# Seven-product blocks that sum in PSUM: ScalarE copies partial sums from bank to bank, TensorE adds onto them, VectorE keeps one addition per block

## The chip, the cores and the metric

The kernel runs on one core of a Trainium2 chip. The metric is the device time of one execution in microseconds. The core has four computing engines with a queue each: TensorE (PE; its weight loads are listed as PEld), VectorE (DVE), ScalarE (ACT) and GpSimd (POOL). SyncE (SP) issues most of the DMAs. Matrix products land in PSUM, which the kernel uses as eight banks of 128 partitions by 512 fp32 numbers; everything else lies in SBUF.

## The reference

A two-layer network on 512 tokens of width 1024. Each layer mixes tokens (layer A by chunked spatial gating, layer B by forgetting attention; both add attention to a memory of 256 rows) and then runs a gated feed-forward part of hidden width 2816 (22 blocks of 128):

```python
for layer in range(DEPTH):
    a = rmsnorm(h, ln_mix_pre[layer])
    ...
    mixed = jnp.concatenate([main, memory_attention(q_mem, mem_n, w_mem_kv[layer])], axis=-1)
    h = h + rmsnorm(mixed @ w_out[layer], ln_mix_post[layer])
    f = rmsnorm(h, ln_ffn_pre[layer])
    f = (jax.nn.silu(f @ w_ffn_gate[layer]) * (f @ w_ffn_up[layer])) @ w_ffn_down[layer]
    h = h + rmsnorm(f, ln_ffn_post[layer])
return h
```

The change is in the two products `f @ w_ffn_gate` and `f @ w_ffn_up`.

## The kernel before

Activations are held transposed: features on the partitions, tokens along the free dimension. An fp32 number is held as two parts, a high one that ScalarE makes by a rounding copy and a low one, the rest, that VectorE makes by a subtraction (`split`, line 239). A product of such pairs is three matmuls (`mm3`, lines 191 to 193): high by high, low weights or low data in the other two.

**Blocks of seven products.** Of the 22 hidden blocks of a layer, the first two are computed plainly. The other 20 go in ten pairs, and each pair is computed once for the gate weights and once for the up weights: 20 times per layer an object of the class `Seven`. It treats its piece of work as a product of 2x2 block matrices: two hidden blocks by two halves of the 1024 input features (the weight quadrants a11, a12, a21, a22, 128x512 each), times two halves of the features by two halves of the tokens. The four results take seven block products in place of eight, with additions before (`sums`: four VectorE additions on the weights; `combined`: the same on the data, once per layer) and additions behind. Each block product is four feature tiles times three matmuls, 12 matmuls with a 128x128 weight tile and 256 tokens.

With P1 to P7 for the products, the first hidden block gets P1 + P2 on the left tokens and P1 + P6 + P5 + P3 on the right ones; the second gets P1 + P6 + P7 + P4 and P1 + P6 + P7 + P5 (kept with the opposite sign, which the next step undoes).

**How the sums are made before.** A block has three PSUM tiles in three banks: `x` (512 wide; P2 in the left half, P3 in the right), `a` (`self.p`, 256 wide, in which P1, P6 and P5 are added up) and `e` (`self.q`, 256 wide; P7, then P4 on top). ScalarE copies four partial sums to SBUF tiles `s1` and `s2`, at lines 1059 (P1), 1074 (P7), 1071 (P1 + P6) and 1068 (P1 + P6 + P5). The products run in the order 1, 7, 2, 6, 4, 3, 5. In `end`, VectorE adds `e` and `a` onto the halves of `s2` (lines 1079 and 1080, 256 wide) and `x` onto `s1` (line 1082, 512 wide), and hands each finished row of 512 to `rows`: `gate_rows` multiplies by the norm factors and applies Silu, `up_rows` multiplies by the gate and splits the result into high and low parts for the down product.

**Where things wait for each other.** PSUM tiles come from pools by tag: `mm` (3 banks, the gate blocks), `lg` (3 banks, the up blocks) and `tr` (2). Weight parts come from a ring of 8 pairs of SBUF tiles (tags `hi` and `lo`); a block needs 7 pairs. The program writes the blocks one after the other; the framework's planner sets each engine's order at build time and the semaphores between engines, and it may put a later instruction ahead of an earlier one. The first pair of each layer (`plain_first`) runs its gate and up blocks interleaved, in the order 1, 2, 3, then 7, 6, then 4, 5. After each group of two or three pairs the down product for that group follows (tiles `y`), with 512-wide matmuls; its weights use the same ring.

Of the kernel before, what the change touches and what calls it, by code (L numbers as in the profile page):

```python
# [11 lines left out]
ALU = mybir.AluOpType  # L12
# [3 lines left out]
P = 128  # L16
# [17 lines left out]
HALVES = ((0, 256), (256, 512))  # L34
FULL = (0, 512)

ORDER = (6, 7, 0, 1, 2, 3, 4, 5)
# [3 lines left out]
def hybrid(ctx: ExitStack, tc: tile.TileContext, i: dict, out: bass.AP):  # L41
# [13 lines left out]
    def name(s):  # L55
        n_of[s] = n_of.get(s, 0) + 1
        return f"{s}_{n_of[s]}"
# [7 lines left out]
    def prob(s, shape=(P, T)):  # L65
        return tp.tile(list(shape), F32, tag="p", name=name(s), bufs=6)
# [7 lines left out]
    def ps(tag, shape=(P, T), s="ps"):  # L74
        return pp.tile(list(shape), F32, tag=tag, name=name(s), bufs=2 if tag == "tr" else 3)

    V, A, PE, G = nc.vector, nc.scalar, nc.tensor, nc.gpsimd
# [160 lines left out]
    def split(src, hi, lo, eng=None):  # L238
        last_parts[:] = A.copy(hi, src), (eng or V).tensor_sub(lo, src, hi)  # L239
# [22 lines left out]
    class Norm:  # L262


        def __init__(self, width=T):
            self.r4 = small("r4")
            self.acc, self.width = None, width
# [750 lines left out]
    class Seven:  # L1018
# [5 lines left out]
        def __init__(self, xs, src, tag, rows):  # L1024
            self.xs, self.rows = xs, rows
            w1, w2 = loaded(src(0)), loaded(src(1))
            self.a = [w[:, d : d + 512] for w in (w1, w2) for d in (0, 512)]
            self.x, self.p = ps(tag, s="x"), ps(tag, (P, 256), s="a")
            self.q = ps(tag, (P, 256), s="e")
            self.s1, self.s2 = prob("s1"), prob("s2")  # L1030

        def parts(self, src):
            pair = pair_of_parts()
# [14 lines left out]
        def product(self, o, w, n, more=False):  # L1048
            for k, w in enumerate(cut(w, P)):
                mm3(o, w, self.xs[n][k], k == 0 and not more, k == KT // 2 - 1, more)  # L1050

        def run(self, what):

            a11, a12, a21, a22 = self.a
            left, right = (slice(*c) for c in HALVES)
            s1, s2 = self.s1, self.s2
            if what == 1:
                self.product(self.p, self.w1, 0)
                A.copy(s1[:, left], self.p)
            elif what == 2:  # L1060
                self.product(self.x[:, left], self.w2, 2)
            elif what == 3:
                self.product(self.x[:, right], self.parts(a12), 5)
            elif what == 4:
                self.product(self.q, self.parts(a22), 4, True)
            elif what == 5:
                self.product(self.p, self.parts(a21), 6, True)
                A.copy(s1[:, right], self.p)
            elif what == 6:
                self.product(self.p, self.parts(a11), 3, True)  # L1070
                A.copy(s2[:, left], self.p)
            else:
                self.product(self.q, self.parts(self.s3), 1)
                A.copy(s2[:, right], self.q)

        def end(self):
            left, right = (slice(*c) for c in HALVES)
            s1, s2 = self.s1, self.s2
            V.tensor_add(s2[:, left], self.q, s2[:, left])
            V.tensor_add(s2[:, right], self.p, s2[:, right])  # L1080
            self.rows(1, s2)
            end = V.tensor_add(s1, self.x, s1)
            self.rows(0, s1)
            ended[0] = end

    ended = [None]

    def sevens(pair, plain_first, opens=False):

        if not plain_first:  # L1090
            for make in pair:
                u = make()
                with behind(ended if opens else ()):
                    u.sums()
                opens = False
                for n in (1, 7, 2, 6, 4, 3, 5):
                    u.run(n)
                u.end()
            return
        us = []  # L1100
        for make in pair:
            us.append(make())
            us[-1].sums()
            for n in (1, 2, 3):
                us[-1].run(n)
        for some in ((7, 6), (4, 5)):
            for u in us:
                for n in some:
                    u.run(n)
        for u in us:  # L1110
            u.end()

    def feed_forward(layer, phase, xp, meanwhile=None):

        nnorm = PairNorm()
        rb = rbc
        groups = ((2, 8), (8, 14), (14, 18), (18, 22))

        def hidden(gate, up, f, cols):
            c0, c1 = cols  # L1120
            n = c1 - c0
            gr = temp("gr")
            V.tensor_mul(gr[:, :n], gate, rb[:, c0:c1])
            s = temp("silu")
            A.activation(s[:, :n], gr[:, :n], AF.Silu)
            ff = temp("f")
            V.tensor_mul(ff[:, :n], up, s[:, :n])
            split(ff[:, :n], f[0][:, c0:c1], f[1][:, c0:c1])

        gates = [None] * 3  # L1130

        def gate_rows(row, g):

            V.tensor_mul(g, g, rb)
            gates[2] = A.activation(g, g, AF.Silu, scale=-1.0 if row else 1.0)
            gates[row] = g

        def up_rows(row, u, fs):
            if row:
                V.scalar_tensor_tensor(out=u, in0=u, scalar=-1.0, in1=gates[1], op0=ALU.mult, op1=ALU.mult)  # L1140
            else:
                V.tensor_mul(u, u, gates[0])
            split(u, *fs[len(fs) - 2 + row])

        fs = [(act("fhi"), act("flo")) for _ in range(2)]

        def first(n, aside):
            return prepared(i["w_up" if n % 2 else "w_gate"][layer, n // 2], (KT, P), aside)

        def evac_first(outs, cols):  # L1150
            for m in range(2):
                hidden(outs[2 * m], outs[2 * m + 1], fs[m], cols)

        scaled = {}
        a, close = boundary(phase, G_MIX_POST + layer, G_FFN_PRE + layer, nnorm, rb, first, evac_first, scaled)
        w = [down_weights(layer, 0, dh) for dh in range(2)]
        close()
        xs, last = combined(a, scaled, xp)
        last()
        ys = [[plain("y") for _ in range(2)] for _ in range(TB)]  # L1160
        for tb in range(TB):
            for dh in range(2):
                o = ps("lg" if dh else "mm", s="y")
                for k in range(2):
                    token_products(o, fs[k], w[dh][k], tb, k == 0, k == 1)
                A.copy(ys[tb][dh], o)

        for gi, (k0, k1) in enumerate(groups):
            fs = []
            for m in range(k0, k1, 2):  # L1170
                if meanwhile and m == k1 - 2 and gi == len(groups) - 1:
                    next(meanwhile)
                fs += [(act("fhi"), act("flo")) for _ in range(2)]
                sevens((lambda: Seven(xs, lambda n: i["w_gate"][layer, m + n], "mm", gate_rows),
                        lambda: Seven(xs, lambda n: i["w_up"][layer, m + n], "lg",
                                      lambda row, t: up_rows(row, t, fs))), m == 2, m == k0)
            nk = k1 - k0
            if gi == len(groups) - 1:
                if layer:
                    with behind([gates[2]]):  # L1180
                        A.preload_act_table_set("natural_log_exp_and_others")
                if meanwhile:
                    next(meanwhile)

                eps = small("eps")
                V.tensor_mul(eps, nnorm.r4, nnorm.r4)
                V.reciprocal(eps, eps)
                V.tensor_scalar_mul(eps, eps, RMS_EPS)
                return tail_of(fs, lambda kp, dh, aside, k0=k0: down_weights(layer, k0 + 2 * kp, dh, aside), ys, eps,
                               layer == 1)  # L1190
            for dh in range(2):
                outs = [ps("mm" if tb < 2 else "lg", s="y") for tb in range(TB)]
                for kp in range(nk // 2):
                    w = down_weights(layer, k0 + 2 * kp, dh)
                    for x in range(2):
                        k = 2 * kp + x
                        for tb in range(TB):
                            token_products(outs[tb], fs[k], w[x], tb, k == 0, k == nk - 1)
                for tb in range(TB):
                    V.tensor_add(ys[tb][dh], outs[tb], ys[tb][dh])  # L1200
# [230 lines left out]
    for tb in range(TB):  # L1431
        end, sums = tail(tb)
# [68 lines left out]
```

## Time and profile before

| | |
|---|---|
| device time, 3 runs | median 1104.92 us (1104.75 to 1105.23) |
| span of the profiled execution | 1102.4 us |
| granted TensorE clock, mean | 0.999 |
| HBM read, written | 105.23 MB, 2.10 MB |
| mean DMA rate | 108 GB/s |

The profiled execution's own time is its span and some 2.5 us around it, going by the median. In the profile's lines a group is named by program line, engine, operation and tiles (`out<-in`), then shape and count, total and mean time, and the idle time of the engine just before, with what ended it. The matmuls of the blocks stand under the helper lines 191 to 193, so they are told apart by tile: `x`, `a` and `e`. A timeline row has start, duration, engine, line and operation; consecutive matmuls overlap in it, since each is listed with its way through the array, so the distance between starts is what a matmul costs.

### The profile page before, as it was taken

Reading aid. Unit: us, or ns where it says so; the run is one execution under the profiler, and the core shown is the slowest. Engines: PE = TensorE matmul, PEld = TensorE weight load, DVE = VectorE, ACT = ScalarE, POOL = GpSimd, SP = SyncE. Lnnn points to the kernel's source line nnn. Section 1 sums busy time; section 2 is a strip of 40 time slices with the busy share of each in tenths; the row PEclk is TensorE's granted clock in tenths of the full one; section 3 lists DMA queues with packets and bytes.
Section 4 is the critical chain, followed back from the end, with each engine's and each line's share of the span. In section 5 each row is a group of like instructions: output and inputs, shape, how many; then the busy total and the mean of one; then the engine's idle time right before and its main releaser. Section 6 shows DMA issues by size and latency. Waiting matters only on the chain.

```text
span 1102.4 us, 19497 instructions
## 1 busy us (share of the span) xinstructions
PE 1094.9 (99%) x7362; PEld 1001.0 (91%) x7363; DVE 887.8 (81%) x1750; ACT 679.7 (62%) x1428; POOL 23.9 (2%) x40
## 2 busy tenths in 40 slices
PE   9999999999999999999999999999999999999998
PEld 8998889999899899998988998889999899899996
DVE  7879759997698488797968789868997698588776
ACT  7776578664365254477747788868665266255454
POOL 0000000000000000001000000000000000000000
PEclk9999999999999999999999999999999999999999
DMA  7521331334135133245222654531235134233232
GB/s 271 160 78 58 115 115 39 116 115 138 54 115 148 53 106 115 77 153 175 73 80 61 154 130 125 148 115 40 78 97 153 58 114 132 62 114 117 77 97 77
DMA packets 64021, 118.65 MB, mean 108 GB/s; under 512 B 5236, under 2 KB 40072, under 8 KB 63928
## 3 DMA queue, kind: packets, MB, share of 16 engines
q1 hardware_dynamic: 63032, 116.57, 34.7%
q8 instruction: 58, 0.95, 0.4%
q0 software_dynamic: 192, 0.52, 0.2%
q10 hardware_dynamic: 704, 0.32, 0.1%
q14 instruction: 35, 0.29, 0.1%
HBM read 105.23 MB, written 2.10 MB: 97 GB/s over the span
## 4 chain that ended last, share of the span: by engine, by line
PE 95%; DVE 2%; ACT 2%; DMA 0%; issue 0%; SPq 0%; DVEq 0%; ACTq 0%
PE y L191 10%; PE y L192 10%; PE y L193 10%; PE a L191 5%; PE a L193 5%; PE a L192 5%; PE ps L191 4%; PE ps L193 4%; PE ps L192 4%; PE e L191 3%; PE e L193 3%; PE e L192 3%; PE x L193 3%; PE x L191 3%; PE x L192 3%; PE v L191 2%
## 5 line engine op out<-in xcount | busy, mean ns | idle before, releaser
L239 ACT CAST whi<-raw 128x512 fp32r<-128x512 f32 x460 | 277.6, 620 | 260.3 <-PE y L193 118.5
L239 DVE TENSOR_TENSOR wlo<-raw,whi 128x512 fp32r<-128x512 f32 x460 | 306.3, 686 | 116.8 <-ACT whi L239 114.7
L191 PE MATMUL y<-whi,fhi 128*128 128x512 f32 (+1 forms) x356 | 139.6, 393 | 0.0
L193 PE MATMUL y<-whi,flo 128*128 128x512 f32 (+1 forms) x356 | 139.4, 391 | 0.0
L192 PE MATMUL y<-wlo,fhi 128*128 128x512 f32 (+1 forms) x356 | 139.2, 391 | 0.0
L193 PE MATMUL x<-xshi,wlo 128*128 128x256 f32 x320 | 89.8, 281 | 0.0
L191 PE MATMUL x<-xshi,whi 128*128 128x256 f32 x320 | 89.7, 280 | 0.0
L191 PE MATMUL a<-xshi,whi 128*128 128x256 f32 x320 | 89.7, 281 | 0.0
L192 PE MATMUL a<-xslo,whi 128*128 128x256 f32 x320 | 89.7, 280 | 0.0
L192 PE MATMUL x<-xslo,whi 128*128 128x256 f32 x320 | 89.7, 280 | 0.0
L193 PE MATMUL a<-xshi,wlo 128*128 128x256 f32 x320 | 89.6, 281 | 0.0
L193 PEld LDWEIGHTS y<-whi,flo 128*128 128x128 f32 x356 | 66.9, 188 | 15.6 <-DVE flo L239 0.2
L192 PEld LDWEIGHTS y<-wlo,fhi 128*128 128x128 f32 x356 | 66.9, 188 | 14.9 <-DVE wlo L239 0.2
L191 PEld LDWEIGHTS y<-whi,fhi 128*128 128x128 f32 x356 | 66.9, 188 | 14.7 <-ACT fhi L239 0.2
L191 PE MATMUL ps<-xshi,whi 128*128 128x256 f32 (+1 forms) x224 | 68.4, 305 | 0.0
L192 PE MATMUL ps<-xslo,whi 128*128 128x256 f32 (+1 forms) x224 | 66.7, 298 | 0.0
L193 PE MATMUL ps<-xshi,wlo 128*128 128x256 f32 (+1 forms) x224 | 66.3, 298 | 0.0
L191 PEld LDWEIGHTS a<-xshi,whi 128*128 128x128 f32 x320 | 60.3, 188 | 0.3
L192 PEld LDWEIGHTS a<-xslo,whi 128*128 128x128 f32 x320 | 60.2, 188 | 0.4
L191 PEld LDWEIGHTS x<-xshi,whi 128*128 128x128 f32 x320 | 60.2, 188 | 0.0
L193 PEld LDWEIGHTS x<-xshi,wlo 128*128 128x128 f32 x320 | 60.2, 188 | 0.0
L193 PEld LDWEIGHTS a<-xshi,wlo 128*128 128x128 f32 x320 | 60.2, 188 | 0.0
(303 smaller groups left out, 3075.1 us busy)
## 6 DMA issues: line engine op xcount, KB each, us to landing
raw<-in_w_gate SPq DMA_DIRECT2D x44, 512.0 KB, 3.6
raw<-in_w_up SPq DMA_DIRECT2D x44, 512.0 KB, 3.6
raw<-in_w_down SPq DMA_DIRECT2D x44, 512.0 KB, 4.0
raw<-in_w_out SPq DMA_DIRECT2D x16, 512.0 KB, 4.0
raw<-in_w_b_q SPq DMA_DIRECT2D x8, 512.0 KB, 4.3
raw<-in_w_a_v SPq DMA_DIRECT2D x6, 512.0 KB, 8.1
raw<-in_w_a_u SPq DMA_DIRECT2D x6, 512.0 KB
raw<-in_w_v SPq DMA_DIRECT2D x6, 512.0 KB, 3.5
```

The source lines that it names most:

```text
L191: PE.matmul(o, w[0], x[0], start=start, stop=False, skip_group_check=more)
L192: PE.matmul(o, w[0], x[1], start=False, stop=False, skip_group_check=more)
L193: return PE.matmul(o, w[1], x[0], start=False, stop=stop, skip_group_check=more)
L239: last_parts[:] = A.copy(hi, src), (eng or V).tensor_sub(lo, src, hi)
```

## The change

A block now has two PSUM tiles in two banks, `r` and `x`, both 512 wide. P1, P6 and P5 add up in the right half of `r`. ScalarE copies the sums from there to where TensorE goes on adding: P1 to the left half of `x` (P2 is added on top), P1 + P6 to the left half of `r` (P4 on top), P1 + P6 + P5 to the right half of `x` (P3 on top). P7 is first computed in the left half of `r` and copied to SBUF (the left half of `s1`). At the end VectorE makes one addition, `r` plus that copy of P7, the latter read twice, for the second row; the first row stands finished in `x`, and `rows` reads it from PSUM. The order of the products becomes 1, 7, 6, 2, 5, 4, 3. The first pair of each layer uses a class of its own, `FirstSeven`, with the sums of before, but on tiles `r` and `x`, and with the two half additions joined into one of 512.

```diff
-            self.x, self.p = ps(tag, s="x"), ps(tag, (P, 256), s="a")
-            self.q = ps(tag, (P, 256), s="e")
+            self.banks(tag)
...
+        def banks(self, tag):
+            self.r, self.x = ps(tag, s="r"), ps(tag, s="x")
...
+        ORDER = (1, 7, 6, 2, 5, 4, 3)
+
         def run(self, what):
...
             if what == 1:
-                self.product(self.p, self.w1, 0)
-                A.copy(s1[:, left], self.p)
+                self.product(r[:, right], self.w1, 0)
+                A.copy(x[:, left], r[:, right])
             elif what == 2:
-                self.product(self.x[:, left], self.w2, 2)
+                self.product(x[:, left], self.w2, 2, True)
             elif what == 3:
-                self.product(self.x[:, right], self.parts(a12), 5)
+                self.product(x[:, right], self.parts(a12), 5, True)
             elif what == 4:
-                self.product(self.q, self.parts(a22), 4, True)
+                self.product(r[:, left], self.parts(a22), 4, True)
             elif what == 5:
-                self.product(self.p, self.parts(a21), 6, True)
-                A.copy(s1[:, right], self.p)
+                self.product(r[:, right], self.parts(a21), 6, True)
+                A.copy(x[:, right], r[:, right])
             elif what == 6:
-                self.product(self.p, self.parts(a11), 3, True)
-                A.copy(s2[:, left], self.p)
+                self.product(r[:, right], self.parts(a11), 3, True)
+                A.copy(r[:, left], r[:, right])
             else:
-                self.product(self.q, self.parts(self.s3), 1)
-                A.copy(s2[:, right], self.q)
+                self.product(r[:, left], self.parts(self.s3), 1, True)
+                A.copy(s1[:, left], r[:, left])
+
+        def end(self):
+            two = lambda t: t.rearrange("p (a b) -> p a b", a=2)
+            V.tensor_add(two(self.s2), two(self.r), self.s1[:, :256].unsqueeze(1).to_broadcast([P, 2, 256]))
+            self.rows(1, self.s2, self.s2)
+            ended[0] = self.rows(0, self.x, self.s1)
+
+    class FirstSeven(Seven):
...
         def end(self):
...
-            V.tensor_add(s2[:, left], self.q, s2[:, left])
-            V.tensor_add(s2[:, right], self.p, s2[:, right])
-            self.rows(1, s2)
-            end = V.tensor_add(s1, self.x, s1)
-            self.rows(0, s1)
-            ended[0] = end
+            V.tensor_add(s2, self.r, s2)
+            self.rows(1, s2, s2)
+            ended[0] = V.tensor_add(s1, self.x, s1)
+            self.rows(0, s1, s1)
...
-                for n in (1, 7, 2, 6, 4, 3, 5):
+                for n in u.ORDER:
                     u.run(n)
...
-        def gate_rows(row, g):
-
-            V.tensor_mul(g, g, rb)
+        def gate_rows(row, src, g):
+
+            end = V.tensor_mul(g, src, rb)
...
-        def up_rows(row, u, fs):
+        def up_rows(row, src, u, fs):
             if row:
-                V.scalar_tensor_tensor(out=u, in0=u, scalar=-1.0, in1=gates[1], op0=ALU.mult, op1=ALU.mult)
+                end = V.scalar_tensor_tensor(out=u, in0=src, scalar=-1.0, in1=gates[1], op0=ALU.mult, op1=ALU.mult)
             else:
-                V.tensor_mul(u, u, gates[0])
+                end = V.tensor_mul(u, src, gates[0])
             split(u, *fs[len(fs) - 2 + row])
+            return end
...
+                Kind = FirstSeven if m == 2 else Seven
```

The fourth argument of `product`, `more`, leaves out the start flag, so that the first matmul adds onto what stands in the bank.

More of the change, by code (lines that the diff above doesn't have):

```diff
@@ L1055, in run @@
             left, right = (slice(*c) for c in HALVES)
-            s1, s2 = self.s1, self.s2
+            x, r, s1 = self.x, self.r, self.s1
             if what == 1:
-                self.product(self.p, self.w1, 0)
-                A.copy(s1[:, left], self.p)
+                self.product(r[:, right], self.w1, 0)
+                A.copy(x[:, left], r[:, right])
             elif what == 2:
-                self.product(self.x[:, left], self.w2, 2)
+                self.product(x[:, left], self.w2, 2, True)
@@ new lines, in end, with run @@
+        def end(self):
[4 more added lines that the diff above has]
+    class FirstSeven(Seven):
+        def run(self, what):
+            a11, a12, a21, a22 = self.a
+            left, right = (slice(*c) for c in HALVES)
+            s1, s2, x, q, p = self.s1, self.s2, self.x, self.r[:, left], self.r[:, right]
+            if what == 1:
+                self.product(p, self.w1, 0)
+                A.copy(s1[:, left], p)
+            elif what == 2:
+                self.product(x[:, left], self.w2, 2)
+            elif what == 3:
+                self.product(x[:, right], self.parts(a12), 5, True)
+            elif what == 4:
+                self.product(q, self.parts(a22), 4, True)
+            elif what == 5:
+                self.product(p, self.parts(a21), 6, True)
+                A.copy(s1[:, right], p)
+            elif what == 6:
+                self.product(p, self.parts(a11), 3, True)
+                A.copy(s2[:, left], p)
+            else:
+                self.product(q, self.parts(self.s3), 1, True)
+                A.copy(s2[:, right], q)
@@ L1130, in feed_forward @@
         gates = [None] * 3
-        def gate_rows(row, g):
-            V.tensor_mul(g, g, rb)
+        def gate_rows(row, src, g):
+            end = V.tensor_mul(g, src, rb)
             gates[2] = A.activation(g, g, AF.Silu, scale=-1.0 if row else 1.0)
             gates[row] = g
-        def up_rows(row, u, fs):
+            return end
+        def up_rows(row, src, u, fs):
             if row:
-                V.scalar_tensor_tensor(out=u, in0=u, scalar=-1.0, in1=gates[1], op0=ALU.mult, op1=ALU.mult)
+                end = V.scalar_tensor_tensor(out=u, in0=src, scalar=-1.0, in1=gates[1], op0=ALU.mult, op1=ALU.mult)
             else:
-                V.tensor_mul(u, u, gates[0])
+                end = V.tensor_mul(u, src, gates[0])
             split(u, *fs[len(fs) - 2 + row])
+            return end
         fs = [(act("fhi"), act("flo")) for _ in range(2)]
@@ L1173, in feed_forward @@
                 fs += [(act("fhi"), act("flo")) for _ in range(2)]
-                sevens((lambda: Seven(xs, lambda n: i["w_gate"][layer, m + n], "mm", gate_rows),
-                        lambda: Seven(xs, lambda n: i["w_up"][layer, m + n], "lg",
-                                      lambda row, t: up_rows(row, t, fs))), m == 2, m == k0)
+                Kind = FirstSeven if m == 2 else Seven
+                sevens((lambda: Kind(xs, lambda n: i["w_gate"][layer, m + n], "mm", gate_rows),
+                        lambda: Kind(xs, lambda n: i["w_up"][layer, m + n], "lg",
+                                     lambda row, src, t: up_rows(row, src, t, fs))), m == 2, m == k0)
             nk = k1 - k0
```

## The prediction, made before the changed kernel was run

> **What bounds the kernel now.** The first view is the page: span, then the busy time of each engine.
>
> ```profile
> span 1102.4 us, 19497 instructions
> PE 1094.9 (99%) x7362; PEld 1001.0 (91%) x7363; DVE 887.8 (81%) x1750; ACT 679.7 (62%) x1428; POOL 23.9 (2%) x40
> PE 95%; DVE 2%; ACT 2%; DMA 0%; issue 0%; SPq 0%; DVEq 0%; ACTq 0%
> ```
>
> TensorE (PE) is busy for all but 7.5 us of the span, and in the chain that ended last it holds 95%. VectorE (DVE) is second with 81%. That share is a mean over stages, so the second view is the table by stretches of time: three of pure feed-forward work, and the end of the kernel.
>
> ```profile
> 202.00:262.00 60.00, 60.00 (x506) 59.86 (x505) 55.21 (x98) 39.94 (x82) 0.00 (x0) 1.00 0.40 125
> 294.60:345.00 50.40, 50.40 (x427) 50.36 (x426) 46.87 (x81) 31.29 (x64) 0.00 (x0) 1.00 0.30 94
> 767.00:1073.00 306.00, 306.00 (x2170) 286.40 (x2170) 247.86 (x428) 161.09 (x317) 0.70 (x1) 1.00 0.32 99
> 1074.00:1102.00 28.00, 23.73 (x128) 19.02 (x128) 18.84 (x46) 13.55 (x33) 1.64 (x3) 0.97 0.26 76
> ```
>
> The columns are length, PE, weight loads, DVE, ScalarE (ACT), POOL, granted clock, DMA. PE has no idle time at all in the stretches that the change touches: 60.00 of 60.00, 50.40 of 50.40, 306.00 of 306.00. DVE has 81 to 93% there, close behind, but behind. A busy PE may still be slowed, so the third view is the timeline of one block of seven products: the first matmul of each, in its old order 1, 7, 2, 6, 4, 3, 5, and the first of the next block.
>
> ```profile
> 241.33 0.29 PE L191 MATMUL a<-xshi,whi 128*128 128x256 f32 x1
> 242.77 0.28 PE L191 MATMUL e<-t3hi,whi 128*128 128x256 f32 x1
> 244.16 0.28 PE L191 MATMUL x<-xshi,whi 128*128 128x256 f32 x1
> 245.58 0.28 PE L191 MATMUL a<-d2hi,whi 128*128 128x256 f32 x1
> 247.00 0.28 PE L191 MATMUL e<-t,whi 128*128 128x256 f32 x1
> 248.41 0.28 PE L191 MATMUL x<-xshi,whi 128*128 128x256 f32 x1
> 249.84 0.28 PE L191 MATMUL a<-xshi,whi 128*128 128x256 f32 x1
> 251.27 0.28 PE L191 MATMUL a<-xshi,whi 128*128 128x256 f32 x1
> ```
>
> Each product of 12 matmuls starts 1.39 to 1.44 us after the one before: 1.42 us, or 0.118 us a matmul, with nothing between. So in a block PE is the limit and does not wait for DVE or ACT. What DVE is spared is worth nothing there; what PE is made to wait is lost in full.
>
> **The change, part by part.** How many blocks: the final addition has 40 rows, one for each block (2 layers, 10 pairs); the first pair of each layer keeps the old scheme, so 36 blocks change.
>
> ```profile
> L1079 DVE TENSOR_TENSOR s<-e,s 128x256 f32<-128x256 f32 x40 | 16.7, 418 | 2.9 <-PE e L193 2.9
> L1080 DVE TENSOR_TENSOR s<-a,s 128x256 f32<-128x256 f32 x40 | 16.7, 417 | 2.3 <-ACT s L1068 2.3
> L1082 DVE TENSOR_TENSOR s<-x,s 128x512 f32<-128x512 f32 x40 | 27.2, 680 | 0.0
> L1134 DVE TENSOR_TENSOR s<-s,rbc 128x512 f32<-128x512 f32 x40 | 25.7, 682 | 0.0
> L1254 DVE TENSOR_TENSOR k<-k,rbc 128x512 f32<-128x512 f32 x6 | 4.1, 686 | 0.4 <-PE k L193 0.2
> ```
>
> *VectorE.* Gone from a block: 0.418 + 0.417 + 0.680 us of additions. New: one 512-wide addition with one input in PSUM, 0.680 as L1082. The first row's multiplication now reads PSUM in place of SBUF: 0.682 against 0.686 (L1254 reads PSUM), no difference. So 0.835 us a block, 36 x 0.835 = 30 us of DVE, and 4 x 0.155 = 0.6 us in the old-style blocks, whose two half additions become one. By the windows this work lies beside a PE that never idles: I cost the gain at 0.
>
> *TensorE.* The same 84 matmuls a block, in the order 1, 7, 6, 2, 5, 4, 3, no cheaper. Cost 0 but for waits.
>
> *ScalarE.* Four copies a block before, four after.
>
> ```profile
> L1071 ACT COPY s<-a 128x256 f32<-128x256 f32 x40 | 14.7, 367 | 4.2 <-PE a L193 4.2
> L1307 ACT ACTIVATE e<-az x1: 233/233/233, 590.7 to 590.7; 128x48 f32<-128x48 f32 x1
> ```
>
> Three of the new ones write PSUM, and no row of this trace has ACT writing PSUM. Bounds: not under 0.23 us (the 48-wide activation), not over the 0.62 us of a 512-wide cast; I take 0.37 from the nearest row.
>
> *The waits: here is the price.* Before, the products went to three banks in turn (a, e, x, a, e, x, a), and a bank that a copy was reading was written again two products later. Now the order goes to banks r, r, r, x, r, r, x, where the halves of r hold different sums but are one tile of the program. Is a write to one half held back while ACT reads the other? The trace has one place of this kind: the first value block of layer B, where ACT reads columns 0 to 255 of a PSUM tile and DVE columns 256 to 267, with no data passing between them.
>
> ```profile
> 584.04 0.47 ACT L1293 ACTIVATE vf<-v,r 128x256 f32<-128x256 f32 x1 [0.52 <-PE v L193]
> 584.55 0.23 DVE L1295 SCALAR_TENSOR_TENSOR z<-v,r,bf 128x12 f32<-128x12 f32 x1 [0.98 <-ACT vf L1293]
> ```
>
> DVE sat idle for 0.98 us until ACT's read ended at 584.51. So two engines on disjoint columns of one PSUM tile are kept apart by a wait, and I expect the same between ACT's copy and PE. The trace has it for two reads; for a PE write no run shows it. (The Trainium skill, page "PSUM — Partial Sum Buffer", section "PSUM bank collisions raise a hardware error", says that any two engines on one bank, at other addresses too, collide with an error, so a program that runs must wait here; by the opposite rule, waits by address, the time would be the unchanged 1104.9.)
>
> That makes PE wait in three places a block: product 7 for copy 1, product 6 for copy 7, product 4 for copy 5. A fourth wait, product 5 for copy 6, has product 2 (1.42 us) between. How long is each, from the moment PE could go on? In the block above, ACT's copies after products 1, 7, 6 and 5:
>
> ```profile
> 242.86 0.62 ACT L239 CAST whi<-raw 128x512 fp32r<-128x512 f32 x1 [0.56 <-PE a L192]
> 243.38 0.37 ACT L1059 COPY s<-a 128x256 f32<-128x256 f32 x1
> ...
> 245.03 0.62 ACT L239 CAST fhi<-s 128x512 fp32r<-128x512 f32 x1
> 245.56 0.37 ACT L1074 COPY s<-e 128x256 f32<-128x256 f32 x1
> ...
> 247.20 0.37 ACT L1071 COPY s<-a 128x256 f32<-128x256 f32 x1 [0.76 <-PE a L193]
> ...
> 251.35 0.62 ACT L239 CAST whi<-raw 128x512 fp32r<-128x512 f32 x1 [0.31 <-PE a L192]
> 251.88 0.37 ACT L1068 COPY s<-a 128x256 f32<-128x256 f32 x1
> ```
>
> Copy 1 ends at 243.75, and product 7 had started at 242.77: 0.98 us. Copy 7: 245.93 - 244.16 = 1.77. Copy 6: 247.57 - 247.00 = 0.57. Copy 5: 252.25 - 251.27 = 0.98. Three of the four stand behind a cast. After products 1 and 5 this is no accident: a product's next-to-last matmul is the last to read its high weights and releases ACT's next cast ("PE a L192") before the last matmul releases the copy. Queued behind each waiting PE instruction is all of PE.
>
> *What fills the waits.* PE's stream is not the program's order: this is the middle of a three-matmul step of a key block.
>
> ```profile
> 591.82 0.40 PE L191 MATMUL k<-shi,whi 128*128 128x512 f32 x1
> 592.06 0.40 PE L192 MATMUL k<-slo,whi 128*128 128x512 f32 x1
> 592.38 0.63 PE L465 MATMUL tr<-ident,mp 128*128 128x128 f32 x4
> 592.77 0.48 PE L193 MATMUL k<-shi,wlo 128*128 128x512 f32 x1
> ```
>
> Four transposes stand between its second and third matmul, so a matmul that is ready is issued ahead of one that is not. In a block, product 2 is ready once copy 1 is done and can fill the wait for copy 7. For the waits for copies 6 and 5 the block has nothing left; there the first product of the next block can go in: its weights are cast one ring ahead (8 pairs of tiles, 7 used per block) and the third bank of its tag is free. Its second product cannot, as it waits for its own copy 1; that copy then falls beside products 4 and 3. A block's sum: 1.77 - 1.42 = 0.35 after copy 7, and 0.57 + 0.98 - 1.42 = 0.13 after copies 6 and 5: 0.48 us, times 36 = 17 us. If copy 6 gets a cast ahead of it too (0.98): 0.35 + 0.54 = 0.89, times 36 = 32 us. I take the rows as they stand. With the copy at its bounds, each of the three waits moves by -0.14 or +0.25 us: down to 0.48 - 0.42 = 0.06 a block, 2 us, or up by 0.75 x 36 = 27 us. (The Trainium skill, page "ScalarE: Activation LUTs", says in "Step-by-step: what each stage is for" that ScalarE writes PSUM with less latency than SBUF; it gives no figure, no run here shows it, and it would pull the sum towards 2 us.)
>
> *PSUM and the rest.* A block takes two banks in place of three; PE waited for none before, so 0. DMAs and queues are unmoved.
>
> **The sum** stands against one execution of 1102.4 us span; the timed runs have a median of 1104.92, so 2.5 us lie around it, taken as unchanged. 1104.9 + 17 = **1122 us**; the forecast's own range goes from 2 us to 17 + 27 us more, 1107 to 1149.
>
> **Rivals.**
> *All covered, no change.* The copies of the new order may be let ahead of the casts, since PE hangs on them; with copies 6 and 7 near 0.57 and copy 5 too, 1.14 us are less than product 1's 1.42. The same follows if halves aren't kept apart. For it: ACT has 62% and can spare the time. Against it: three of four copies stand behind a cast. It gives 1105.
>
> *Nothing is taken from the next block.* Then copies 1, 6 and 5 are paid in full and copy 7 in part: 0.98 + 0.57 + 0.98 + 0.35 = 2.88 us, x 36 = 104 us: 1209. Against it: the key block's rows.
>
> *Faster.* DVE, 0.835 us a block lighter, comes out of each layer's last pair earlier by 2 x 0.835 = 1.7 us, and what follows the feed-forward part begins that much sooner; the last 28 us show PE idle for 4.3. Both layers: 3.3 us, 1101.6. It decides only where DVE is late when the tail's products end, and there it waits for PE:
>
> ```profile
> DVE y L846 <- PE y L193: 18.2, 16, 2.1
> ```
>
> Sixteen waits of the tail's additions, 18.2 us in all, for PE: DVE is early. So this is unlikely.
>
> **How the numbers follow.** Forecast 0.55, all covered 0.25, nothing taken 0.14, faster 0.06. The range leaves out the last two (0.20) and takes in the other two: 1103 to 1150. A measurement of this kernel can tell about 0.2%, 2 us, from no change; so faster 0.06, same 0.25, slower 0.69.
>
> **What would show it.** Right: in the windows of the feed-forward part PE is less than fully busy, or its products lie more than 1.42 us apart; the list of waits has PE or its weight loads held by ACT copies; PE's order has the next block's first product between 6 and 5 or 5 and 4; DVE's busy time falls by some 30 us with nothing to show for it. Wrong: products at 1.42 us throughout (all covered, or halves not kept apart), or products 1 and 7 of one block next to each other with a gap of about 1 us in every block (nothing taken).

## The result, and the profile after

The changed kernel takes 1147.61 us (median of 4 runs, 1146.8 to 1148.2) against 1104.84 us before: a ratio of 1.0388, 95% interval 1.0373 to 1.0403. That is 42.8 us more, where 17 were forecast. The page of the changed kernel, the lines that answer to those of before:

```profile
span 1146.2 us, 19421 instructions
...
PE 1124.3 (98%) x7362; PEld 1008.7 (88%) x7363; DVE 869.2 (76%) x1674; ACT 680.4 (59%) x1428; POOL 24.0 (2%) x40
...
PE 91%; ACT 4%; DVE 3%; issue 1%; DMA 1%; SPq 0%; ACTq 0%; DVEq 0%
```

The same 7362 matmuls, less DVE work, and ACT and DVE now hold 7% of the chain that ended last. The windows of the feed-forward parts (length, PE, weight loads, DVE, ACT, POOL, clock, DMA) show idle PE where there was none:

```profile
204.50:265.00 60.50, 57.89 (x463) 55.47 (x462) 50.98 (x83) 36.59 (x75) 0.00 (x0) 1.00 0.37 114
...
801.00:1110.00 309.00, 302.09 (x2052) 273.79 (x2051) 223.73 (x360) 151.34 (x296) 0.00 (x0) 1.00 0.32 98
```

2.6 of 60.5 us and 6.9 of 309. That is less than what is missing, since a matmul's row covers its way through the array and hides short waits. The list of waits names the releasers (total us, times, longest):

```profile
PEld r L191 <- ACT x L1063: 11.8, 18, 1.3
PEld r L191 <- ACT x L1072: 11.1, 24, 0.7
...
PE r L191 <- ACT x L1063: 8.0, 12, 1.1
...
PE r L191 <- ACT x L1072: 4.8, 14, 0.5
...
PEld r L191 <- ACT r L1075: 3.3, 16, 0.3
...
PEld r L191 <- ACT s L1078: 1.4, 8, 0.2
```

L1063 is the copy after product 1, L1072 after 5, L1075 after 6, L1078 after 7. All four copies hold PE up, through the weight load (PEld) of the next product in bank `r`.

For a full account I took the start of each of the 3360 matmuls of the blocks in the timeline, and the start of PE's next one. Undisturbed they are 0.118 us apart; where the distance is more than 0.025 us over that, the excess counts as a stall. Before, there is no such stall in any block. Now they sum to 40.8 us. The two spans differ by 43.8 us; of the 3.0 us left, 2.0 lie at matmuls outside the blocks and the rest in distances under that limit. By the matmul that is late:

| late | times | us |
|---|---|---|
| first matmul of product 7 (waits for copy 1) | 18 | 11.0 |
| first of product 4 (copy 5) | 29 | 8.9 |
| first of product 5 (copy 6) | 29 | 2.9 |
| first of product 6 (copy 7) | 20 | 2.4 |
| the matmul behind a held one, 0.10 us each on average | 138 | 14.1 |
| product 1 (low weights from DVE, and others) | 8 | 1.5 |

The four blocks of the first pairs, which aren't among the 36, hold some 1.2 us of this.

**A wait for copy 1, as the timeline shows it.** Product 1 of a block had 11 of its 12 matmuls done between products 2 and 4 of the block before. The last one stood behind that block's products 4 and 3:

```profile
325.00 0.28 PE L193 MATMUL x<-xshi,wlo 128*128 128x256 f32 x1
...
325.11 0.28 PE L193 MATMUL r<-xshi,wlo 128*128 128x256 f32 x1
...
325.19 0.62 ACT L239 CAST whi<-raw 128x512 fp32r<-128x512 f32 x1 [0.79 <-PE x L192]
325.23 0.28 PE L191 MATMUL r<-xshi,whi 128*128 128x256 f32 x1
...
325.34 0.28 PE L192 MATMUL r<-xslo,whi 128*128 128x256 f32 x1
325.72 0.37 ACT L1063 COPY x<-r 128x256 f32<-128x256 f32 x1
...
326.13 0.19 PEld L191 LDWEIGHTS r<-t3hi,whi 128*128 128x128 f32 x1 [0.72 <-ACT x L1063]
326.14 0.39 PE L191 MATMUL r<-t3hi,whi 128*128 128x256 f32 x1 [0.52 <-ACT x L1063]
326.24 0.19 PEld L192 LDWEIGHTS r<-t3lo,whi 128*128 128x128 f32 x1
326.36 0.28 PE L192 MATMUL r<-t3lo,whi 128*128 128x256 f32 x1
```

At 325.00 product 3 starts its last matmul. At 325.11 comes the one matmul that product 1 has left, and only now can its copy go. It stands behind a cast, runs from 325.72 to 326.09, and product 7 starts at 326.14. PE fits in two matmuls of the block after next (325.23, 325.34); the third, the first that reads that block's low weights, stands later in its order, at 330.68. The last four rows show the second cost: product 7's first weight load starts together with its matmul (326.13, 326.14) and not some 0.12 us ahead, so the matmul lasts 0.39 us in place of 0.28, and the next starts 0.22 us later, not 0.118.

**VectorE and ScalarE.** The addition that is left, and the three copies that now write PSUM beside the one that still writes SBUF:

```profile
L1082 DVE TENSOR_TENSOR s<-r,s 128x512 f32<-128x512 f32 x36 | 24.9, 692 | 29.3 <-PE r L193 29.3
...
L1075 ACT COPY r<-r 128x256 f32<-128x256 f32 x36 | 13.2, 366 | 1.8 <-PE r L193 1.8
L1072 ACT COPY x<-r 128x256 f32<-128x256 f32 x36 | 13.2, 366 | 2.1 <-PE r L193 2.1
L1078 ACT COPY s<-r 128x256 f32<-128x256 f32 x36 | 13.0, 362 | 0.1
L1063 ACT COPY x<-r 128x256 f32<-128x256 f32 x36 | 12.9, 358 | 0.0
```

The copies cost 0.36 to 0.37 us wherever they go. (The Trainium skill, page "ScalarE: Activation LUTs", section "Step-by-step: what each stage is for", gives PSUM the lower latency as ScalarE's target; here the difference is within 0.01 us.) DVE is busy 18.6 us less, and now waits 29.3 us for PE before its addition.

### The profile page after: what moved, and what is told of

Read it like the earlier page. It is cut to its first block, busy times and chain, and to the rows that moved or that the text cites. A ratio compares the mean times of both kernels' runs of the same rounds, so it can differ in the third digit from the quotient of the medians.

```text
span 1146.2 us, 19421 instructions
## 1 busy us (share of the span) xinstructions
PE 1124.3 (98%) x7362; PEld 1008.7 (88%) x7363; DVE 869.2 (76%) x1674; ACT 680.4 (59%) x1428; POOL 24.0 (2%) x40
## 4 chain that ended last, share of the span: by engine, by line
PE 91%; ACT 4%; DVE 3%; issue 1%; DMA 1%; SPq 0%; ACTq 0%; DVEq 0%
PE r L191 10%; PE y L191 10%; PE y L192 10%; PE y L193 10%; PE r L192 7%; PE r L193 7%; PE ps L191 4%; PE ps L193 4%; PE ps L192 4%; PE x L192 3%; PE x L191 3%; PE x L193 3%; PE v L191 2%; PE v L192 2%; PE v L193 2%; PE tr L465 1%
## 5 line engine op out<-in xcount | busy, mean ns | idle before, releaser
L239 DVE TENSOR_TENSOR wlo<-raw,whi 128x512 fp32r<-128x512 f32 x460 | 310.5, 687 | 150.0 <-ACT whi L239 143.6
L191 PE MATMUL r<-xshi,whi 128*128 128x256 f32 x320 | 93.7, 293 | 0.2
L193 PE MATMUL r<-xshi,wlo 128*128 128x256 f32 x320 | 89.7, 283 | 0.2
L192 PE MATMUL r<-xslo,whi 128*128 128x256 f32 x320 | 89.7, 281 | 0.0
L191 PEld LDWEIGHTS r<-xshi,whi 128*128 128x128 f32 x320 | 60.2, 188 | 6.5 <-ACT r L1075 3.3
L193 PEld LDWEIGHTS r<-xshi,wlo 128*128 128x128 f32 x320 | 59.9, 188 | 1.4 <-DVE wlo L239 1.4
L192 PEld LDWEIGHTS r<-xslo,whi 128*128 128x128 f32 x320 | 60.3, 188 | 0.4
L192 PEld LDWEIGHTS x<-xslo,whi 128*128 128x128 f32 x320 | 60.3, 188 | 0.0
```

What stands on the lines that cost most here:

```text
L191: PE.matmul(o, w[0], x[0], start=start, stop=False, skip_group_check=more)
L192: PE.matmul(o, w[0], x[1], start=False, stop=False, skip_group_check=more)
L193: return PE.matmul(o, w[1], x[0], start=False, stop=stop, skip_group_check=more)
```

## The experiments

Theory A: the copies and the next products share bank `r`, so PE waits; what counts is which work stands behind each copy. Theory B: copying into PSUM, or adding onto what ScalarE wrote, is what costs. "Stalls" are counted as above, in the trace of each kernel; edits are against the changed kernel.

### Three banks: the halves of r apart

```diff
-            self.r, self.x = ps(tag, s="r"), ps(tag, s="x")
+            self.x, self.p, self.q = ps(tag, s="x"), ps(tag, (P, 256), s="p"), ps(tag, (P, 256), s="q")
...
-                A.copy(r[:, left], r[:, right])
+                A.copy(q, p)
...
-            V.tensor_add(two(self.s2), two(self.r), self.s1[:, :256].unsqueeze(1).to_broadcast([P, 2, 256]))
+            for c, o in zip(HALVES, (self.q, self.p)):
+                V.tensor_add(self.s2[:, slice(*c)], o, self.s1[:, :256])
...
```

> The changed kernel, but the halves of r are two tiles in two banks (p for products 1, 6, 5; q for 7 and 4), so a block takes three banks as before and has two 256-wide additions again; copies into PSUM and the order stay. The marks that say whether a matmul adds onto or overwrites a column aren't kept up in the right half of x, so the sums of the first row may lack a part; the instructions are the same. Theory A (PE waits because a copy and the next product share bank r): every wait now has a product of 1.42 us between, against a copy that ends 0.6 to 1.8 us late; stalls inside the blocks fall from 41 us to under 6: 1105 to 1111. Theory B (the copies into PSUM, or adding onto what ScalarE wrote, cost by themselves): stays above 1135.

Measured: 1113.72 us, ratio 1.0082 (1.0067 to 1.0097). Stalls fall from 40.8 to 8.1 us, and those of a first matmul held by a copy alone to 1.4 us (6 times). The list of PE's waits has no copy near its top any more; what is left is DVE (total us, times, longest):

```profile
PEld p L193 <- DVE wlo L239: 4.1, 8, 0.6
...
PE p L193 <- DVE wlo L239: 2.4, 8, 0.4
...
PE x L191 <- ACT x L1072: 0.2, 1, 0.2
```

So the copies into PSUM and the order of products are nearly free with the halves in two banks; theory B falls. The time is 2.7 us over the expected range. The rest is mostly new: eight times product 1's low weights come 0.4 to 0.6 us late from DVE. The trace shows what they stand behind on DVE:

```profile
316.40 0.69 DVE L1179 SCALAR_TENSOR_TENSOR s<-s,s 128x512 f32<-128x512 f32 x1
...
316.55 0.62 ACT L239 CAST whi<-raw 128x512 fp32r<-128x512 f32 x1 [0.79 <-PE x L192]
...
317.00 0.68 DVE L1181 TENSOR_TENSOR s<-x,s 128x512 f32<-128x512 f32 x1
...
317.60 0.68 DVE L239 TENSOR_TENSOR wlo<-raw,whi 128x512 fp32r<-128x512 f32 x1
...
318.33 0.19 PEld L193 LDWEIGHTS p<-xshi,wlo 128*128 128x128 f32 x1 [0.50 <-DVE wlo L239]
```

The cast ends at 317.17, but DVE first makes both rows of the up block just finished (L1179, L1181) and starts the subtraction at 317.60. All eight look like this, with some 0.43 us between (once 0.56). And the kernel, with 36 blocks lighter on DVE, is still 8.9 us slower than before.

The edit parts two things at once, the bank and the tile: each tile here has a bank of its own. So it does not show whether the planner keeps `r`'s halves apart because they share a bank or because they are one tile of the program. This kernel also doesn't keep up the marks in `x`, so a part of the first row's sums is lost: its time is evidence, not a version to use.

### The shared bank alone

```diff
     class FirstSeven(Seven):
+        ORDER = (1, 7, 2, 6, 4, 3, 5)
...
-                Kind = FirstSeven if m == 2 else Seven
+                Kind = FirstSeven
```

> The changed kernel with the class FirstSeven for all blocks, in the order of before (1, 7, 2, 6, 4, 3, 5): copies go to SBUF as before and only the shared bank r stays. Theory A: product 7 waits for copy 1, 6 for copy 7, 4 for copy 6, but products 2 and 3 depend on no copy and can fill; what is left is mostly the 0.1 us by which the second matmul after each wait is late: 36 x 3 x 0.105 = 11 us and some rest, 1113 to 1130. Theory B: no copy into PSUM, so 1105.

Measured: 1126.43 us, ratio 1.0199 (1.0184 to 1.0214), within the range of theory A. In the changed blocks nothing writes PSUM but TensorE here, and half of the loss is there. The copies that hold PE up are now those of `FirstSeven`, after products 1 (L1098), 6 (L1110) and 7 (L1113):

```profile
PEld r L191 <- ACT s L1110: 4.5, 17, 0.8
PEld r L191 <- ACT s L1113: 4.0, 18, 0.8
PEld r L191 <- ACT s L1098: 2.5, 14, 0.2
```

Of 20.6 us of stalls, 10.1 are first matmuls of products 7, 6 and 4 and 10.6 are the matmul behind them, 0.1 us each (110 times). Products 2 and 3, free of copies in this scheme, fill most of the waits, but each short one that remains also makes the matmul behind it late.

### Gate and up blocks in turn

```diff
-                for n in u.ORDER:
+            for n in Seven.ORDER:
+                for u in us:
                     u.run(n)
+            for u in us:
                 u.end()
```

> The changed kernel, but the products of a pair's gate block and up block take turns (1, 1, 7, 7, 6, 6 and so on). Theory A: behind each copy stands the other block's product, 1.42 us, longer than the 0.98 us of a copy behind a cast; stalls fall under 10 us: 1105 to 1115. Theory B: the same copies and banks, so it stays at about 1148.

Measured: 1126.11 us, ratio 1.0195 (1.0180 to 1.0211): above the range of theory A, well under that of B. The late matmuls behind a held one fall from 138 to 38, so a product of 1.42 us behind a copy does end most waits early. But 20.2 us of stalls are left, 15.2 of them in 27 waits of products 7 and 4, nearly all for copies. The timeline of ACT before one of them, at the start of a pair:

```profile
318.44 0.60 ACT L239 CAST whi<-raw 128x512 fp32r<-128x512 f32 x1
318.95 0.61 ACT L239 CAST fhi<-s 128x512 fp32r<-128x512 f32 x1
319.47 0.61 ACT L239 CAST whi<-raw 128x512 fp32r<-128x512 f32 x1
319.99 0.61 ACT L239 CAST fhi<-s 128x512 fp32r<-128x512 f32 x1
320.51 0.36 ACT L1063 COPY x<-r 128x256 f32<-128x256 f32 x1
```

Both blocks of a pair now end together, their rows reach ACT in one burst, and copy 1 of the next pair stands behind four casts, until 320.87; product 7 starts at 320.92, 1.05 us late. There 1.42 us of cover is too little. I had counted the cover, not the queue in front of the copy.

### Casts held behind the copies

```diff
-            split(src, *pair)
+            with behind([self.copied[after]] if after in self.copied else ()):
+                hi = A.copy(pair[0], src)
+            V.tensor_sub(pair[1], src, pair[0])
...
-                self.product(r[:, left], self.parts(a22), 4, True)
+                self.product(r[:, left], self.parts(a22, 5), 4, True)
```

(and in the same way for products 2, 7 and 5; `self.copied` holds the copies of the block before)

> The changed kernel, but the cast of weights that a product's end releases is held behind the copy that the same end releases (casts for products 2, 7, 5 and 4 of a block behind the copies 1, 7, 6 and 5 of the block before). Theory A with the cast as a part of it: copies that stood behind a cast start 0.5 us sooner; of the 11.0 us before product 7 some 9 go, of the 8.8 us before product 4 some 7; the 0.105 us after each wait (14 us) stays: 1128 to 1136. If a cast ahead of the copy is not what makes the waits long: 1145 to 1150.

Measured: 1155.13 us, ratio 1.0455 (1.0438 to 1.0472): slower than the changed kernel, outside both ranges. A part of the expectation held: the stall before product 4 fell from 8.9 to 5.3 us, its median from 0.31 to 0.19 us, as copy 5 is out sooner; 7 us had been expected to go. But product 7 was late 28 times, not 18, and for 14.9 us in place of 11.0:

```profile
PEld r L191 <- ACT x L1067: 18.4, 34, 1.3
PEld r L191 <- ACT x L1076: 8.6, 33, 0.4
```

(L1067 is copy 1 here, L1076 copy 5.) Fewer matmuls of the next block's product 1 are taken into the shorter waits: in 18 blocks six of its 12 stay behind product 3, where in the changed kernel a single one does in eight. So copy 1 lacks cover in more blocks. Product 6's stalls rose too, from 2.4 to 5.3 us, and the matmuls late behind a held one from 138 to 168 (17.5 us). This suggested the next two.

### Nothing of the next block is pulled ahead

```diff
-                self.product(r[:, right], self.w1, 0)
+                with behind(third):
+                    self.product(r[:, right], self.w1, 0)
...
-                self.product(x[:, right], self.parts(a12), 5, True)
+                third[:] = [self.product(x[:, right], self.parts(a12), 5, True)]
```

> The changed kernel, but product 1 of a block is held behind the last matmul of the block before, so that nothing of the next block fills a wait. Theory A (waits on the shared bank, shortened by pulled work): copies 1, 6 and 5 are paid in full (0.98 + 0.57 to 0.98 + 0.98 us), of copy 7 some 0.1, and four times 0.105 us for the held weight load: 3.0 to 3.5 us a block, 36 blocks, 108 to 126 us over 1105: 1213 to 1231. If the pulled work was worth little: 1150 to 1170.

Measured: 1203.60 us, ratio 1.0890 (1.0872 to 1.0908), 98.6 us over before; some 10 us under the range, mainly since 26 to 28 of the 36 blocks pay copies 1, 5 and 6, not all. The waits that the pulled product 1 had filled:

```profile
PEld r L191 <- ACT x L1067: 34.5, 28, 1.6
PEld r L191 <- ACT x L1076: 31.6, 35, 1.1
PEld r L191 <- ACT r L1079: 18.6, 32, 1.1
```

Copy 1 (L1067), copy 5 (L1076) and copy 6 (L1079) each cost what the timeline of before had shown: the stalls' medians are 1.08, 1.02 and 0.56 us against 0.98, 0.98 and 0.57 worked out there. What the planner pulls ahead is worth 56 us.

### Product 1 of the next block first

```diff
...
-                for n in u.ORDER:
+                u.run(1)
+                settle((4, 3))
+                for n in (7, 6, 2, 5):
                     u.run(n)
-                u.end()
+                pend.append(u)
```

(`settle` runs the named products and the `end` of the pending block; it is also called once at the end of a group)

> The changed kernel, but the program names the next block's product 1 ahead of this block's products 4 and 3, so that none of its 12 matmuls is left over behind product 3. Theory A with the left-over as the cause of the waits before product 7: those (11.0 us, and 1.9 for the weight load behind them) go, the waits before 4, 5 and 6 stay (14 us and 11): 1130 to 1138. If the waits before product 7 come from ScalarE being late by itself: 1144 to 1150.

Measured: 1130.33 us, ratio 1.0230 (1.0215 to 1.0245), as expected of the left-over. The stalls before product 7 go from 11.0 to 1.0 us (8 times), all stalls from 40.8 to 23.9. Little is left of the wait that led PE's list in the changed kernel:

```profile
PEld r L191 <- ACT x L1063: 1.2, 7, 0.2
```

The copies and the bank are the same. The planner's order changed elsewhere too: the stalls before products 4, 5 and 6, which were to stay at 14 us, fell to 10.4, with product 4's down from 8.9 to 3.1.

### A product of another bank behind each copy

```diff
...
-                for n in u.ORDER:
+                u.run(1)
+                for p in pend:
+                    p.run(4)
+                u.run(7)
+                settle((3,))
+                for n in (6, 2, 5):
                     u.run(n)
-                u.end()
+                pend.append(u)
```

> The changed kernel, same banks and copies, but the program's order goes across blocks: 1 of the next block, 4, 7 of the next, 3, then 6, 2, 5 of the next, so that behind each copy but copy 7 (behind it product 3) and copy 6 (product 2) a product of another bank stands. Theory A: every copy has 1.42 us of cover, more than the 0.98 us of a copy behind a cast: under 10 us of waits, and no late weight load where the wait ended early: 1106 to 1116. If sharing the bank costs in itself, whatever stands between: above 1125, as with the gate and up blocks in turn.

Measured: 1120.05 us, ratio 1.0130 (1.0113 to 1.0147), 4 us over the range of theory A. 13.1 us of stalls are left. Within a group of pairs there are none over long stretches, as the first matmuls of three products in a row show:

```profile
316.07 0.28 PE L191 MATMUL r<-xshi,whi 128*128 128x256 f32 x1
...
317.50 0.28 PE L191 MATMUL r<-t,whi 128*128 128x256 f32 x1
...
318.90 0.28 PE L191 MATMUL r<-t3hi,whi 128*128 128x256 f32 x1
...
320.32 0.28 PE L191 MATMUL x<-xshi,whi 128*128 128x256 f32 x1
```

1.40 to 1.43 us each, as before the change, all with the shared bank and the copies into PSUM. What remains sits at the first blocks of a group, which have no block before them, and where a copy is late on ACT, up to 0.9 us. It is the fastest of the orders tried on two banks, and slower than the kernel before.

## Why the prediction was right or wrong

**Right.** That PE was the limit and DVE's relief worth nothing: DVE is 18.6 us less busy and the kernel slower. (The 30 us were over-sized, in part because rows that follow each other closely on DVE overlap in the list: 0.68 us long, 0.60 apart. It had no effect.) That the halves of `r` are kept apart: with three banks nearly all waits go. (The Trainium skill, page "PSUM — Partial Sum Buffer", section "PSUM bank collisions raise a hardware error", asks to keep engines apart by bank and not by address; this agrees as far as a wait can, and no run here shows a collision.) That copies take 0.37 us. That product 2 and the next block's product 1 are pulled into the waits: without the latter it is 56 us more. The rival "nothing is taken" was priced at 1209 where 1203.6 was measured, which is in part luck: the price had 0.35 us a block for copy 7, where 0.11 was measured, and nothing for the held weight loads, where it was 0.41. The direction was right. That 1147.6 lies inside the range of 1103 to 1150 is luck: the upper part of the range stood for copies of 0.62 us, and they took 0.36 to 0.37.

**Wrong**, in the step "what fills the waits" and the sum drawn from it, 0.48 us a block (17 us) against 40.8 / 36 = 1.13. The rows below add up to 1.10; the rest is the 1.5 us of product 1.

| term, us a block | predicted | measured |
|---|---|---|
| copy 7, behind product 2 | 0.35 | 2.4 / 36 = 0.07 |
| copies 6 and 5, behind product 1 of the next block | 0.13 | 11.8 / 36 = 0.33 |
| copy 1, "beside products 4 and 3" | 0 | 11.0 / 36 = 0.31 |
| weight load held back at each wait | not in the sum | 14.1 / 36 = 0.39 |

The largest term was left out. I took the copy's end as the moment at which PE goes on at full pace; the wait sits on the weight load, so each held product loses 0.105 us more, however short its wait. The second failure is copy 1. I put product 1 whole into the waits for copies 6 and 5 and so gave its copy the cover of products 4 and 3. In eight blocks a single one of its matmuls stayed behind product 3, in two blocks five, and then copy 1 lacks cover: 7.5 of the 11.0 us. The rest falls on eight blocks that begin a group or follow a first pair, where no such products of a block before stand behind product 1; the sum took all 36 blocks as alike. That more cover for one wait takes it from another is shown twice: shorter waits made it worse (1155), and naming product 1 first took away 10 of these 11 us (1130). The mistake was to treat a filler as all or nothing. The other two terms were mis-sized. Copy 6 stands right behind a cast in 33 of the 36 blocks, which the prediction gave only as its higher case (0.54 a block with copy 5; 0.33 measured). It did so in 31 of 40 blocks before the change too; the one block whose timeline the prediction took for all was one of the others. In the changed kernel:

```profile
241.90 0.62 ACT L239 CAST whi<-raw 128x512 fp32r<-128x512 f32 x1 [1.71 <-issue]
242.43 0.37 ACT L1075 COPY r<-r 128x256 f32<-128x256 f32 x1
```

Copy 7 was over-sized: it ends 0.97 us after product 7 (median), not 1.77, and seven or eight of product 2's twelve matmuls nearly cover it.

**Open.** The 2.0 us outside the blocks; why the planner puts DVE's row operations ahead of product 1's low weights in the three-bank kernel; whether it goes by bank or by tile; whether a version on two banks could get the first blocks of a group covered as well. None of the runs points to a version that beats the kernel before, whose blocks had no stall to begin with.

## What to carry to other kernels

Where TensorE runs without a gap, fewer VectorE additions buy nothing, and a PSUM bank saved can cost more than they are worth: where halves are kept apart as here, ask of every copy out of a bank which matmul next writes that bank, either half of it, and what stands between. Hold the cover against the time from the product's end to the end of its copy, with the queue in front of the copy, and add about 0.1 us for each product that is held at all, as measured here. When work pulled ahead fills a wait, look for its last instruction: what depends on it waits for that one, however much was done early.

## What the runs showed of the hardware

A wait costs TensorE more than its length. In this kernel a weight load normally starts some 0.12 us ahead of its matmul, beside the matmul in front. When the load itself is held by a semaphore, it starts together with its matmul, which takes 0.38 to 0.39 us in place of 0.28, and the following matmul is some 0.105 us late (0.100 to 0.114 in 124 of 138 cases, less in the others), after a wait of 1.2 us as after one of 0.07. Why the load isn't ahead then, no run tells. A product of the block at 240 us in the changed kernel, held 0.08 us:

```profile
240.05 0.28 PE L192 MATMUL x<-xslo,whi 128*128 128x256 f32 x1
240.24 0.19 PEld L191 LDWEIGHTS r<-d2hi,whi 128*128 128x128 f32 x1
240.25 0.38 PE L191 MATMUL r<-d2hi,whi 128*128 128x256 f32 x1
240.35 0.19 PEld L192 LDWEIGHTS r<-d2lo,whi 128*128 128x128 f32 x1
240.47 0.28 PE L192 MATMUL r<-d2lo,whi 128*128 128x256 f32 x1
```

From 240.05 to 240.47 are two steps that take 0.24 us when nothing is held; here 0.42.
